# Sixteen working tiles lengthened by 32 bytes, so that they begin at different places modulo 512 bytes

## The chip, the cores and the metric

The kernel runs on one core of one Trainium2 chip. The metric is the device time of one execution in microseconds (us). Before the change it is 1171.81 us, the median of three runs (1171.26 to 1171.84). One further execution was taken with the hardware profiler; the rows below come from it.

## The reference

Two layers of a streaming encoder over 512 tokens of width 1024, in single precision. Layer 0 mixes tokens with differential attention, layer 1 with gated linear attention; both also attend to 256 memory tokens. Each layer ends in a gated MLP with a causal convolution:

```
for i in range(DEPTH):
    h = rms_norm(x, attn_norm[i])
    proj = h @ (w_in_diff or w_in_gla)
    mix = diff_attention(...) or gla_attention(...)
    cross = memory_cross_attention(mem_q, mem, ...)
    x = x + concatenate([mix, cross]) @ w_out[i]
    h = rms_norm(x, ffn_norm[i])
    x = x + (silu(g) * a) @ w_down[i]     # a, g: halves of conv(h @ w_up[i])
```

What matters here are the dense products: the input projection, the output projection, `h @ w_up` and the product with `w_down`.

## The kernel before, in words

**Split operands.** Every dense product is made of three matmuls. An operand is written as a rounded part `hi` (type fp32r) and the rest `lo`, and hi·hi + hi·lo + lo·hi is summed in one PSUM bank. `split` (L305) makes the pair of an activation, with ScalarE for `hi` and VectorE for `lo`; `split_weights` (L226) that of a weight tile.

**Which operand is loaded and which moves.** A matmul loads 128 columns of one operand into the array and lets up to 512 columns of the other move through.

- `gemm` (L327 to L329), the input projections: the loaded operand is a 128-column slice of the split tokens `xh[k]` or `xl[k]`; the weights `whi`, `wlo` move, 256, 272 or 512 columns wide. L507 is the same, written out for the first projection.
- `product` (L348 to L350), the output projection and the up projection: the loaded operand is a slice of the weights, and the tokens or the mixers' output move, 512 columns wide.
- the step of `down` (L1173), the down projection, done by a scheme of seven products: the loaded operand is a weight slice, and a middle tile of 256 columns moves. Two of the seven kinds of middle operand, b11 and t1, are made with `split_tiles()` and so lie in an x2 tile (`x` in the rows); the others are the pool tiles `midh`, `midl`.

**The x2 tiles.** Pool `xs` holds sixteen buffers with the tag `x2`, each two rows of 512 words a partition (4096 bytes): `pair` (L170) hands out the two rows, `split_tiles` (L174) gives one as `hi` and one as `lo`. Split tokens, split outputs of the mixers, the memory tokens, some operands of the linear attention, b11 and t1, and, from `load_x` (L1056), the residual stream `xT` all live there. In rows of the profile every one of them is called `x`. Beside them the pool has five tiles `xt`; pool `wp` has six `raw`, five `whi` and five `wlo` tiles of 4096 bytes, and the middle tiles have rows of 1024 bytes. Since all these sizes are multiples of 512 bytes, all these tiles begin at byte 416 modulo 512 of a partition, and so do their slices of 128 words. Exceptions are four weight tiles used once at the start (448), the constants `C` (128), the memory's keys and values (320), tiles of the linear attention with rows of 768 or 384 bytes, and the 272-column weight slices of one projection, which lie 1088 bytes apart.

**What sets the order.** TensorE's order is the program's own (`manual_schedule` at L162): attention and linear attention are written as steps, and `Filler` puts pieces of the dense products between them. Weights come as 128x1024 tiles on SP's queue two pieces or five tiles ahead, are split by ScalarE and VectorE, and are read by TensorE. The MLPs are dense products alone.

Of the kernel before, what the change touches and what calls it, by code (L numbers as in the profile page):

```python
# [11 lines left out]
F32 = mybir.dt.float32  # L12
# [9 lines left out]
S = 512  # L22
# [9 lines left out]
X2, XS, EM = 16, 5, 7  # L32
# [118 lines left out]
def trunk(ctx, tc, head_d, x_t, mem_t, wpack, cols_a_d, cols_d, conv_d, gate_d, rel_bias, diff_lambda, consts, onehot, out):  # L151
# [5 lines left out]
    xs = ctx.enter_context(tc.tile_pool(name="xs", bufs=1))  # L157
# [6 lines left out]
    def bank(tag):  # L164
        return ps.tile([128, 512], F32, name=f"ps_{tag}", tag=tag)

    def xtile():
        return xs.tile([128, S], F32, name="xt", tag="xs", bufs=XS)

    def pair(dt=F32):  # L170
        t = xs.tile([128, 2, S], dt, name="x2", tag="x2", bufs=X2)
        return t[:, 0], t[:, 1]

    def split_tiles(pool=None, tag=None, bufs=None):  # L174
        if pool is None:
            return pair(F32R)
        return (pool.tile([128, S], F32R, name=tag + "h", tag=tag, bufs=bufs),
                pool.tile([128, S], F32R, name=tag + "l", tag=tag, bufs=bufs))
# [174 lines left out]
    xT, xpair = [None] * KT, [None] * (KT // 2)  # L353
# [53 lines left out]

    tables("natural_log_exp_and_others")
    memT = [*pair(), *pair()]
    first = [bank("mm"), bank("mm"), bank("sm"), bank("sm")]  # L410

# [23 lines left out]
    with tc.tile_pool(name="ini", bufs=1) as ip, tc.manual_schedule(engines={E.Activation, E.DVE, E.Pool, E.SP}):  # L435
        idle = ip.tile([128, 512], F32, name="idle")
        rb = ip.tile([32, 6], F32, name="rb")
        oh = ip.tile([32, 640], F32, name="oh")
        bs = pair()
        bs = bs[0][:6], bs[1][:6, :128]  # L440
        lv = xtile()[:, :256]
        G.memset(idle, 0.0)
        p = bank("tp")
# [183 lines left out]
    def diff_layer(pool, mix, acc):  # L627
# [129 lines left out]
        for t in range(28):  # L757
# [15 lines left out]
            if t == 16:  # L773
                load_x(x_t)
                out_proj(0, mix, 0, None)
# [34 lines left out]
    def gla_layer(pool, mix, acc):  # L810
# [215 lines left out]
        for h in range(4):  # L1026
            scores(h)
            past_scores(h, 0)
            F.fill(f)
            past_scores(h, 1)  # L1030
            turn_keys(h)
            if h < 3:
                decays(h + 1)
            F.fill(f)
            states(h, 0)
            states(h, 1)
            if h < 3:
                products(h + 1)
            F.fill(f)
            if h == 2:  # L1040
                gate(0)
            outputs(h, 0)
            outputs(h, 1)
            group_norm(pool, o_[h], NB, 1, 192, True)
            F.fill(f)
            if h == 2:
                finish(0)
                load_x(xres)
                out_proj(1, mix, 0, None)
# [6 lines left out]
    def load_x(src):  # L1056
        for k in range(KT):
            if k % 2 == 0:
                xpair[k // 2] = xs.tile([128, 2, S], F32, name="x2", tag="x2", bufs=X2)
            xT[k] = xpair[k // 2][:, k % 2]  # L1060
            nc.sync.dma_start(xT[k], src[k])

# [319 lines left out]
```

## Time and profile before

| | before |
|---|---|
| median of 3 runs | 1171.81 us |
| profiled execution, its own time | 1170.8 us |
| its span, first to last instruction | 1168.9 us |
| TensorE busy with matmuls | 1155.8 us, 6448 matmuls |
| VectorE, ScalarE busy | 886.6 us, 599.2 us |
| DMA engines' mean share | 31.7% on the one busy queue |

How to read it: PE is TensorE's matmuls, PEld its weight loads, which overlap them; DVE is VectorE, ACT ScalarE, SP the queue that issues DMAs. L348 is line 348 of the kernel. `ps_mm<-x,whi 128*128 128x512` is a matmul that writes a bank `mm` from an x2 tile and a weight tile, 128 partitions by 128 loaded columns, 512 columns wide. A matmul's own duration (some 390 ns at 512 columns) says little, since the next one starts before it ends; what counts is the distance between starts.

### The profile page before, as it was taken

To read this page: it belongs to the slowest core of one execution; us is meant where nothing else is said; L and a number is where in the kernel's file an instruction comes from. 1 tells how busy PE (TensorE), PEld (TensorE's weight loads), DVE (VectorE), ACT (ScalarE), POOL (GpSimd) and SP (SyncE) were. 2 spreads that over 40 slices of the span, in tenths; PEclk is the share of its full clock that TensorE was granted. 3 is DMA by queue.
4 is the path that set the end of the run, shared out by engine and by line. 5 is a ranking of instruction groups with operands and counts; after the bars stand their busy time and mean duration, and the time that the engine had idled before them with its cause. 6 is when DMAs were issued, how large, how long until landed. Compare 5 with 4: busy or idle time off the path is not lost.

```text
span 1168.9 us, 16705 instructions
## 1 busy us (share of the span) xinstructions
PE 1155.8 (99%) x6448; PEld 988.7 (85%) x6448; DVE 886.6 (76%) x1454; ACT 599.2 (51%) x1048; POOL 4.1 (0%) x17
## 2 busy tenths in 40 slices
PE   9999999999999999999999999999999999999998
PEld 6887777788898889988998788988889988998888
DVE  7747687679886778668897746868998677876885
ACT  6856677566444444344467534536654344434441
POOL 0000000000000000000000000000000000000000
PEclk9999999999999999999999999999999999999999
DMA  9432213143225222522253221144221632253212
GB/s 313 162 97 90 68 55 127 59 129 97 64 70 182 91 73 72 162 93 70 66 169 112 73 73 46 55 153 126 86 68 64 189 99 73 72 155 98 72 37 73
DMA packets 39853, 117.94 MB, mean 101 GB/s; under 512 B 4735, under 2 KB 7608, under 8 KB 39774
## 3 DMA queue, kind: packets, MB, share of 16 engines
q1 hardware_dynamic: 39630, 116.62, 31.7%
q8 instruction: 51, 0.84, 0.3%
q14 instruction: 28, 0.23, 0.1%
q10 hardware_dynamic: 144, 0.26, 0.1%
HBM read 112.65 MB, written 4.21 MB: 100 GB/s over the span
## 4 chain that ended last, share of the span: by engine, by line
PE 91%; DVE 6%; ACT 2%; issue 1%; DMA 0%; DVEq 0%; ACTq 0%
PE ps_lg L1173 10%; PE ps_mm L348 9%; PE ps_mm L349 9%; PE ps_mm L350 9%; PE ps_sm L350 7%; PE ps_sm L348 7%; PE ps_sm L349 7%; PE ps_mm L327 5%; PE ps_mm L329 5%; PE ps_mm L328 5%; PE ps_tp L1173 5%; PE ps_mm L1173 3%; PE ps_tp L196 2%; PE ps_lg L686 1%; PE ps_sm L722 1%; DVE wlo L230 1%
## 5 line engine op out<-in xcount | busy, mean ns | idle before, releaser
L230 DVE TENSOR_TENSOR wlo<-raw,whi 128x1024 fp32r<-128x1024 f32 (+4 forms) x164 | 186.5, 1140 | 86.5 <-ACT whi L227 85.7
L227 ACT CAST whi<-raw 128x1024 fp32r<-128x1024 f32 (+4 forms) x164 | 160.7, 985 | 155.6 <-PE ps_sm L349 69.9
L348 PE MATMUL ps_mm<-x,whi 128*128 128x512 f32 x438 | 172.6, 394 | 0.3 <-DVE midh L1264 0.3
L349 PE MATMUL ps_mm<-x,whi 128*128 128x512 f32 x438 | 170.6, 389 | 0.2 <-DVE x L309 0.2
L350 PE MATMUL ps_mm<-x,wlo 128*128 128x512 f32 x438 | 170.6, 390 | 0.0
L348 PE MATMUL ps_sm<-x,whi 128*128 128x512 f32 x378 | 148.0, 392 | 0.0
L349 PE MATMUL ps_sm<-x,whi 128*128 128x512 f32 x378 | 147.1, 389 | 0.0
L350 PE MATMUL ps_sm<-x,wlo 128*128 128x512 f32 x378 | 147.1, 389 | 0.0
L327 PE MATMUL ps_mm<-whi,x 128*128 128x512 f32 (+2 forms) x336 | 132.0, 393 | 0.0
L329 PE MATMUL ps_mm<-whi,x 128*128 128x512 f32 (+2 forms) x336 | 126.6, 377 | 0.5 <-DVE x L309 0.4
L328 PE MATMUL ps_mm<-wlo,x 128*128 128x512 f32 (+2 forms) x336 | 125.9, 375 | 0.0
L263 ACT CAST whi<-raw 128x1024 fp32r<-128x1024 f32 (+1 forms) x60 | 58.3, 978 | 86.7 <-PE ps_sm L349 26.2
L348 PEld LDWEIGHTS ps_mm<-x,whi 128*128 128x128 f32 x438 | 82.3, 188 | 17.4 <-issue 0.9
L350 PEld LDWEIGHTS ps_mm<-x,wlo 128*128 128x128 f32 x438 | 82.2, 188 | 17.1
L349 PEld LDWEIGHTS ps_mm<-x,whi 128*128 128x128 f32 x438 | 82.3, 188 | 17.0 <-DVE x L309 0.6
L265 DVE TENSOR_TENSOR wlo<-raw,whi 128x1024 fp32r<-128x1024 f32 (+1 forms) x60 | 67.9, 1131 | 25.2 <-ACT whi L263 25.1
L349 PEld LDWEIGHTS ps_sm<-x,whi 128*128 128x128 f32 x378 | 71.0, 188 | 15.1 <-issue 0.5
L348 PEld LDWEIGHTS ps_sm<-x,whi 128*128 128x128 f32 x378 | 71.0, 188 | 15.0 <-issue 0.5
L350 PEld LDWEIGHTS ps_sm<-x,wlo 128*128 128x128 f32 x378 | 70.9, 188 | 14.8
L1173 PE MATMUL ps_lg<-midh,whi 128*128 128x256 f32 x264 | 75.0, 284 | 1.8 <-DVE x L1178 1.8
L1173 PE MATMUL ps_lg<-midl,whi 128*128 128x256 f32 x264 | 74.7, 283 | 0.0
L1173 PE MATMUL ps_lg<-midh,wlo 128*128 128x256 f32 x264 | 74.7, 283 | 0.0
(308 smaller groups left out, 2287.2 us busy)
## 6 DMA issues: line engine op xcount, KB each, us to landing
raw<-in_wpack_dram SPq DMA_DIRECT2D x170, 512.0 KB, 3.6
raw<-in_wpack_dram SPq DMA_DIRECT2D x24, 384.0 KB, 3.1
x<-in_x_t_dram SPq DMA_DIRECT2D x15, 256.0 KB, 5.2
xres<-x SPq DMA_DIRECT2D x8, 256.0 KB, 3.7
x<-xres SPq DMA_DIRECT2D x8, 256.0 KB, 5.1
raw<-in_wpack_dram SPq DMA_DIRECT2D x7, 256.0 KB, 5.4
bt<-bias_d SPq DMA_DIRECT2D x6, 256.0 KB, 4.9
x<-in_mem_t_dram SPq DMA_DIRECT2D x4, 256.0 KB, 6.1
```

The costliest lines, as they stand in the source:

```text
L196: nc.tensor.transpose(dst, src, ident[:n, :n])
L227: ins = A.copy(hi[:, c], raw[:, c])
L230: V.tensor_sub(lo[:, c], raw[:, c], hi[:, c].bitcast(F32))
L263: A.copy(hi[:, c], raw[:, c])
L265: todo = [lambda: V.tensor_sub(lo[:, c], raw[:, c], hi[:, c].bitcast(F32)), lambda: [sum_weights((*key[:3], *x)) for x in after]]
L327: mm(p, sh[k][:, blk(b)], hi, start=k == 0, stop=False)
L328: mm(p, sh[k][:, blk(b)], lo, start=False, stop=False)
L329: mm(p, sl[k][:, blk(b)], hi, start=False, stop=k == KT - 1)
L348: mm(p, hi[:, blk(n)], bh, start=i == first, stop=False)
L349: mm(p, hi[:, blk(n)], bl, start=False, stop=False)
L350: mm(p, lo[:, blk(n)], bh, start=False, stop=i == last)
L1173: mm(o, a[:, ws], b, start=start and (k, n, i) == (0, 0, 0), stop=k == last and i == 2, skip_group_check=True)
```

## The change

The sixteen x2 tiles get eight words more, 32 bytes, which nothing reads or writes. The view with two rows is cut from the first 1024 words, so each user sees the same shapes; `load_x`, which made such a tile by hand, uses the same function now.

```
     def xtile():
         return xs.tile([128, S], F32, name="xt", tag="xs", bufs=XS)

+    def two_tiles(dt=F32):
+        t = xs.tile([128, 2 * S + 8], dt, name="x2", tag="x2", bufs=X2)
+        return t[:, :2 * S].rearrange("p (a b) -> p a b", a=2)
+
     def pair(dt=F32):
-        t = xs.tile([128, 2, S], dt, name="x2", tag="x2", bufs=X2)
+        t = two_tiles(dt)
         return t[:, 0], t[:, 1]
...
     def load_x(src):
         for k in range(KT):
             if k % 2 == 0:
-                xpair[k // 2] = xs.tile([128, 2, S], F32, name="x2", tag="x2", bufs=X2)
+                xpair[k // 2] = two_tiles()
             xT[k] = xpair[k // 2][:, k % 2]
             nc.sync.dma_start(xT[k], src[k])
```

Buffer n of the sixteen then begins 32n bytes later than before: the sixteen begin at 416, 448, 480, 0, 32 and so on to 384 modulo 512 bytes, each at one place. Everything behind them moves by 16 x 32 = 512 bytes and keeps its place modulo 512. No instruction is added, left out or moved: on each of the five engines the same instructions stand in the same order, and only the line numbers behind the new function are four higher. The pools take 512 bytes more of each partition.

More of the change, by code (lines that the diff above doesn't have):

```diff
@@ L168, in xtile, with two_tiles @@
         return xs.tile([128, S], F32, name="xt", tag="xs", bufs=XS)
+    def two_tiles(dt=F32):
+        t = xs.tile([128, 2 * S + 8], dt, name="x2", tag="x2", bufs=X2)
+        return t[:, :2 * S].rearrange("p (a b) -> p a b", a=2)
     def pair(dt=F32):
-        t = xs.tile([128, 2, S], dt, name="x2", tag="x2", bufs=X2)
+        t = two_tiles(dt)
         return t[:, 0], t[:, 1]
@@ L1058, in load_x @@
             if k % 2 == 0:
-                xpair[k // 2] = xs.tile([128, 2, S], F32, name="x2", tag="x2", bufs=X2)
+                xpair[k // 2] = two_tiles()
             xT[k] = xpair[k // 2][:, k % 2]
```

## The prediction

> **What bounds the kernel now.** I read the head of the page and its busy times first, then the clock and the chain of work that ended last.
>
> ```profile
> span 1168.9 us, 16705 instructions
> PE 1155.8 (99%) x6448; PEld 988.7 (85%) x6448; DVE 886.6 (76%) x1454; ACT 599.2 (51%) x1048; POOL 4.1 (0%) x17
> ...
> core 0: 1168.9 us, clock 1.000
> ...
> PE 91%; DVE 6%; ACT 2%; issue 1%; DMA 0%; DVEq 0%; ACTq 0%
> ```
>
> TensorE is at work from one end to the other, at the full clock, and nine tenths of the chain that sets the end are its own instructions. So the span is the number of matmuls times the distance from one to the next, and that distance is what a change of addresses could touch. "Mean ns of one" does not give it, because matmuls overlap. I take it from starts. First the chain in order of time (start, us, what, count), in the down projection, whose matmuls are 256 columns wide:
>
> ```profile
> 1021.42 8.64 PE ps_lg L1173 x72
> ```
>
> 72 matmuls in 8.64 us are 120.0 ns each. Now TensorE's timeline in the up projection, 512 columns wide, where no row shows an idle time (first and last of a run of 85 matmuls):
>
> ```profile
> 381.38 0.39 PE L348 MATMUL ps_mm<-x,whi 128*128 128x512 f32 x1
> ...
> 400.42 0.39 PE L348 MATMUL ps_mm<-x,whi 128*128 128x512 f32 x1
> ```
>
> 84 distances in 19.04 us: 226.7 ns. The 256 extra columns cost 106.7 ns, so a column costs 0.417 ns, 512 columns 213.3 ns and 256 columns 106.7 ns. Both widths leave the same remainder, **13.3 ns per matmul**, 32 columns' worth. Every matmul has its weight load (6448 of each in the busy row), 128 columns deep; the remainder does not grow with the moving width, so it belongs to the load or to the change of weights. That is what the edit aims at.
>
> **The change part by part.** It removes and adds no instruction, and each engine's order is the same. Sixteen tiles of 4096 bytes become 4128 bytes, so tile n begins 32n bytes later. By the program's layout all sixteen, and whi, wlo and the mid tiles, begin at byte 416 modulo 512 before; after it the mid and weight tiles still do, and the x2 tiles stand at all sixteen multiples of 32. The halves of a tile (2048 bytes apart) and 128-column slices (512 bytes) keep their tile's place.
>
> How many matmuls have one operand in such a tile? The busiest groups, one row of each set:
>
> ```profile
> L348 PE MATMUL ps_mm<-x,whi 128*128 128x512 f32 x438 | 172.6, 394 | 0.3 <-DVE midh L1264 0.3
> ...
> L348 PE MATMUL ps_sm<-x,whi 128*128 128x512 f32 x378 | 148.0, 392 | 0.0
> ...
> L327 PE MATMUL ps_mm<-whi,x 128*128 128x512 f32 (+2 forms) x336 | 132.0, 393 | 0.0
> ...
> L1173 PE MATMUL ps_tp<-x,whi 128*128 128x256 f32 x176 | 32.3, 283 | 0.0
> L1173 PE MATMUL ps_lg<-x,whi 128*128 128x256 f32 x176 | 32.2, 283 | 0.0
> L1173 PE MATMUL ps_tp<-x,wlo 128*128 128x256 f32 x88 | 24.9, 283 | 0.0
> L1173 PE MATMUL ps_lg<-x,wlo 128*128 128x256 f32 x88 | 24.9, 283 | 0.0
> ```
>
> Lines 348 to 350 have the same counts, so 3 x (438 + 378) = 2448; lines 327 to 329 give 3 x 336 = 1008; the down projection 176 + 176 + 88 + 88 = 528. Together **3984**; the first projection (L507) and a few others add under 4% and are left out. One nanosecond per matmul is 4.0 us.
>
> What is a matmul's distance worth when its two streams begin at different places? The dense stages of before never show it, so I bound it by the two nearest stretches.
>
> First, the narrow projection of layer 1. Its weight pieces are 272 columns wide, so the slices begin 0, 1088 and 2176 bytes into whi: 0, 64 and 128 modulo 512 away from the x2 tile they meet.
>
> ```profile
> 611.59 0.29 PE L327 MATMUL ps_mm<-whi,x 128*128 128x272 f32 x1
> ...
> 614.48 0.29 PE L329 MATMUL ps_mm<-whi,x 128*128 128x272 f32 x1
> ```
>
> 24 matmuls, 23 distances, 2.89 us: 125.7 ns. 272 columns are 113.3 ns, so the remainder is 12.3 ns, 1.0 ns less than at equal places. This is the lower bound for places that have been seen: -1.0 ns.
>
> Second, a run just after TensorE has done something else (transposes or single-precision products). The places are equal, but the streams meet at another moment:
>
> ```profile
> 90.58 0.40 PE L328 MATMUL ps_mm<-wlo,x 128*128 128x512 f32 x1
> ...
> 92.89 0.39 PE L329 MATMUL ps_mm<-whi,x 128*128 128x512 f32 x1
> ```
>
> Eleven matmuls, ten distances, 2.31 us: 231.0 ns, 4.3 ns more than in the settled run, with no idle time between them. So the distance does depend on how the two streams stand to each other, and 226.7 ns is a state into which the kernel settles. With one place for all tiles every matmul repeats the last one's pattern; with another place every three matmuls (hi and lo of one tile serve three) it may not settle. Upper bound: +4.3 ns.
>
> The bounds are -1.0 and +4.3 ns. The stretches differ from the dense stages in width or in what ran before, neither is nearer, so I take the middle, **+1.65 ns**: 3984 x 1.65 = +6.6 us.
>
> [...]
>
> The other engines touch the same tiles. An operand at another place is in the trace: the first four raw tiles stand at byte 448 modulo 512.
>
> ```profile
> L230 DVE TENSOR_TENSOR wlo<-raw,whi 128x512 fp32r<-128x512 f32 x7 | 4.8, 681 | 0.0
> ...
> L1140 DVE TENSOR_TENSOR midl<-w,midh 128x512 fp32r<-128x512 f32 x22 | 15.1, 688 | 0.0
> L1140 DVE TENSOR_TENSOR x<-w,x 128x512 fp32r<-128x512 f32 x22 | 15.0, 683 | 0.7 <-ACT x L1137 0.7
> ```
>
> 681 against 683 and 688 ns: nothing, or 1% of operations that lie beside TensorE's matmuls (DVE has 6% of the chain; 1% of that is 0.7 us at most, either way). I take 0. The loads and stores of these tiles:
>
> ```profile
> x<-in_x_t_dram SPq DMA_DIRECT2D x15, 256.0 KB, 5.2
> xres<-x SPq DMA_DIRECT2D x8, 256.0 KB, 3.7
> x<-xres SPq DMA_DIRECT2D x8, 256.0 KB, 5.1
> ```
>
> Bytes, order and queue stay, the tiles were at no rounder place before (416), and DMA has 0% of the chain. Only the first seven loads of x have little cover, since TensorE waits for the first operands; half a microsecond either way is within the range. No wait is added anywhere.
>
> The profiled execution took 1170.8 us, 1.9 us around its span, and 1.0 us less than the median of 1171.8. So 1170.8 + 6.6 = 1177.4 us by the profile's own execution, **1178.4 us** as a median.
>
> **The rivals.**
>
> A, the forecast: the pattern is disturbed, each matmul costs -1.0 to +4.3 ns more; slower in most of that span, up to 1171.8 + 3984 x 4.3 ns = 1188.9 us. For it: 231.0 beside 226.7 ns. Against: the 272-wide stage, with places that do change, is no dearer.
>
> B, the place does not matter. The remainder is the same 32 columns at two widths, as a fixed price of changing weights would be, and 12.3 ns at mixed places is close to 13.3. Then nothing moves: 1171.8 us. [...]
>
> C, the other side: reads that begin at the same place collide, and apart they don't. Place: every matmul above. Price: what remains without collision. The nearest row is a transpose, whose operands begin 288 bytes apart (identity at 128, em at 416):
>
> ```profile
> 143.50 0.93 PE L196 MATMUL ps_tp<-C,em 128*128 128x128 f32 x7
> ...
> L196 PE MATMUL ps_tp<-C,em 128*128 128x128 f32 x92 | 14.0, 273 | 0.0
> ```
>
> (930 - 273) / 6 = 109.5 ns; a single-precision pass goes at two steps a column, and 2 x 128 x 0.417 is 106.7, so 2.8 ns remain. Relief is then 13.3 - 2.8 = 10.5 ns. With fifteen of sixteen places relieved that is 3984 x 15/16 x 10.5 = 39 us, 1133 us; if only the odd multiples of 32 are (the 272-wide stage has seen 64 and 128 and found no relief), 3984 x 8/16 x 10.5 = 21 us, 1151 us. It decides where two streams at full rate share something that repeats within 512 bytes. For it: the remainder is the same at 256 and 512 columns, as a collision over the 128 columns of a load would be. Against: 11 of these 13 ns stay at 64 and 128 bytes, and a run that meets at another moment costs more, never less.
>
> **How the numbers follow.** A 0.43 (0.07 of it above 1190, if a pattern that never settles is dearer than 231 ns), B 0.28, C 0.29 (0.10 of it below 1150). I count as no change what lies within 0.2%, 2.3 us, about what a measurement of this kernel tells from nothing. Likeliest is A at 1178.4 us. The range reaches up to 1190 (the upper bound) and down to 1150 (C with half the places relieved); it leaves out 0.17. Since it holds both signs: A's own range is 1174 to 1190. Faster 0.29, within 0.2% 0.28, slower 0.43.
>
> **What would show it.** After the change the chain's L1173 rows with mid operands must stay at 120.0 ns, since none of their operands moves: they are a control. A: the dense L348 run shows 227 to 231 ns, uneven from tile to tile; B: 226.7 ns as before; C: 216 to 222 ns. If those distances stand still and the time moves, I was wrong about the place, and DVE, ACT or the loads are to be read. The prediction is wrong altogether if distances fall at most places, for then the settled state of before was a collision and not the best one.

## The result and the profile after

The changed kernel takes 1187.80 us, the median of four runs (1187.64 to 1187.92); the kernel before took 1171.53 us beside it (four runs, 1170.90 to 1171.84). The ratio is **1.0137, with an interval of 1.0125 to 1.0150**: slower, by 16.3 us where 6.6 were forecast. The profiled execution took 1187.64 us, 1.8 us around its span.

The head of the page, and the shares of the chain that ended last:

```profile
span 1185.8 us, 16705 instructions
PE 1172.7 (99%) x6448; PEld 987.6 (83%) x6448; DVE 887.6 (75%) x1454; ACT 598.8 (51%) x1048; POOL 4.1 (0%) x17
...
PE 87%; DVE 8%; ACT 2%; DMA 1%; issue 1%; SPq 0%; DVEq 0%; ACTq 0%
```

The span grew by 16.9 us and PE's busy time by as much, 1155.8 to 1172.7 us, with the same 6448 matmuls. DVE (886.6 to 887.6) and ACT (599.2 to 598.8) did the same work in the same time. The groups that the forecast put at nothing did stay there (lines behind the new function are four higher; out<-in, shapes, count, busy us, mean ns; then the loads of the tokens):

```profile
L1144 DVE TENSOR_TENSOR x<-w,x 128x512 fp32r<-128x512 f32 x22 | 15.1, 684 | 0.7 <-ACT x L1141 0.7
```

```profile
x<-in_x_t_dram SPq DMA_DIRECT2D x15, 256.0 KB, 5.2
xres<-x SPq DMA_DIRECT2D x8, 256.0 KB, 3.7
```

683 ns became 684, and 5.2 and 3.7 us are what they were. So the time is in the distances between matmuls. TensorE's timeline in the up projection, whose weights are loaded while the x2 tiles move, first and last of a run of 130 matmuls with no idle time:

```profile
379.77 0.40 PE L353 MATMUL ps_mm<-x,whi 128*128 128x512 f32 x1
...
409.82 0.40 PE L353 MATMUL ps_mm<-x,whi 128*128 128x512 f32 x1
```

129 distances in 30.05 us: **232.9 ns** where it was 226.7. And the chain in the down projection (start, us, what, count): first the 48 matmuls whose middle operand is an x2 tile, then 24 whose middle operand lies in a middle tile:

```profile
456.61 2.83 PE ps_lg L1177 x24
459.44 2.84 PE ps_tp L1177 x24
462.28 2.87 PE ps_mm L1177 x24
465.14 2.88 PE ps_lg L1177 x24
```

2.88 us for 24 is 120.0 ns, the control that had to stand still. The x2 rows have 2.83 and 2.84, 118 ns: at 256 columns the new places are *better*. The row of 2.87 is where the one pattern passes into the other.

Summing all distances between one matmul's start and the next one's, by kind, from the two traces (us; each matmul's distance is the time to the next start):

| kind | matmuls | before | after | ns each |
|---|---|---|---|---|
| `product`, 512 columns, x2 moves (L352 to L354) | 2448 | 559.9 | 574.4 | +5.92 |
| `gemm`, 512 columns, x2 loaded (L331 to L333) | 864 | 204.8 | 207.4 | +3.06 |
| `gemm`, 272 and 256 columns, x2 loaded | 192 | 25.7 | 25.6 | -0.7 |
| down projection, 256 columns, x2 moves | 528 | 63.5 | 62.5 | -1.98 |
| down projection, middle tiles move (control) | 1319 | 160.8 | 161.0 | +0.2 |
| first projection (L511) | 96 | 22.4 | 23.4 | +10.9 |
| all others | 1000 | 126.1 | 125.9 | -0.2 |

Together +16.9 us, all of the span's difference. The first projection's 1.0 us is hardly the change's: it is there, by 1.0 and 1.1 us, in the runs midshift and mid192 below too, which leave these tiles where they were, so it seems that this one profile of before began faster.

### The profile page after: what moved, and what is told of

Read it like the earlier page. It is cut to its first block, busy times and chain, and to the rows that moved or that the text cites. A ratio compares the mean times of both kernels' runs of the same rounds, so it can differ in the third digit from the quotient of the medians.

```text
span 1185.8 us, 16705 instructions
## 1 busy us (share of the span) xinstructions
PE 1172.7 (99%) x6448; PEld 987.6 (83%) x6448; DVE 887.6 (75%) x1454; ACT 598.8 (51%) x1048; POOL 4.1 (0%) x17
## 4 chain that ended last, share of the span: by engine, by line
PE 87%; DVE 8%; ACT 2%; DMA 1%; issue 1%; SPq 0%; DVEq 0%; ACTq 0%
PE ps_mm L353 9%; PE ps_mm L352 9%; PE ps_mm L354 9%; PE ps_lg L1177 8%; PE ps_sm L353 8%; PE ps_sm L354 8%; PE ps_sm L352 8%; PE ps_mm L331 5%; PE ps_mm L332 5%; PE ps_mm L333 5%; PE ps_tp L1177 4%; PE ps_mm L1177 2%; PE ps_tp L200 2%; DVE wlo L269 1%; PE ps_lg L690 1%; PE ps_sm L726 1%
## 5 line engine op out<-in xcount | busy, mean ns | idle before, releaser
L352 PE MATMUL ps_mm<-x,whi 128*128 128x512 f32 x438 | 174.7, 399 | 0.1
L353 PE MATMUL ps_mm<-x,whi 128*128 128x512 f32 x438 | 173.3, 396 | 0.2 <-DVE x L313 0.2
L354 PE MATMUL ps_mm<-x,wlo 128*128 128x512 f32 x438 | 173.2, 395 | 0.0
L352 PE MATMUL ps_sm<-x,whi 128*128 128x512 f32 x378 | 150.0, 397 | 0.0
L354 PE MATMUL ps_sm<-x,wlo 128*128 128x512 f32 x378 | 149.5, 395 | 0.0
L353 PE MATMUL ps_sm<-x,whi 128*128 128x512 f32 x378 | 149.5, 395 | 0.0
L331 PE MATMUL ps_mm<-whi,x 128*128 128x512 f32 (+2 forms) x336 | 132.9, 396 | 0.0
L333 PE MATMUL ps_mm<-whi,x 128*128 128x512 f32 (+2 forms) x336 | 127.4, 379 | 0.5 <-DVE x L313 0.4
L352 PEld LDWEIGHTS ps_mm<-x,whi 128*128 128x128 f32 x438 | 82.3, 188 | 19.7 <-issue 0.6
L354 PEld LDWEIGHTS ps_mm<-x,wlo 128*128 128x128 f32 x438 | 82.2, 188 | 19.5
L352 PEld LDWEIGHTS ps_sm<-x,whi 128*128 128x128 f32 x378 | 71.0, 188 | 17.4 <-issue 0.5
L354 PEld LDWEIGHTS ps_sm<-x,wlo 128*128 128x128 f32 x378 | 70.9, 188 | 16.9
```

What stands on the lines that cost most here:

```text
L331: mm(p, sh[k][:, blk(b)], hi, start=k == 0, stop=False)
L333: mm(p, sl[k][:, blk(b)], hi, start=False, stop=k == KT - 1)
L352: mm(p, hi[:, blk(n)], bh, start=i == first, stop=False)
L353: mm(p, hi[:, blk(n)], bl, start=False, stop=False)
L354: mm(p, lo[:, blk(n)], bh, start=False, stop=i == last)
```

## The experiments

The forecast's reason was that a pattern is lost when the place changes every three matmuls. The theories set against each other, named by these letters where an expectation names them:

- **T1**, the forecast's: a *change* of place from tile to tile unsettles the stream. A constant difference costs nothing.
- **T2**: the distance depends on *how far apart* the moving and the loaded operand begin, and equal places are the good ones at 512 columns. Changing from tile to tile adds little.
- **T3**: it takes the traffic of the other engines or the DMAs to the same tiles.
- **T4**, the forecast's rival C: equal places collide. It had fallen for 512 columns with the result, but the down projection points its way.

**Run mb: the disputed cost by itself.** Behind the kernel before, 17 runs of 48 matmuls at 512 columns (96 at 256) on tiles that nothing else touches, at a time when the other engines are done. The pattern is the kernel's: hi·hi, hi·lo, lo·hi on one tile, then the next tile.

```
+        zero, step = lambda k: 0, lambda k: 8 * k % 128        # words
+        runs = (("warm", 512, zero, zero), ("a", 512, zero, zero),
+            ("b", 512, lambda k: 8, zero), ("c", 512, lambda k: 16, zero), ("d", 512, lambda k: 32, zero),
+            ("e", 512, lambda k: 64, zero), ("f", 512, step, zero), ("g", 512, zero, step), ("h", 512, step, step),
+            ("i", 512, lambda k: 64 * (k % 2), zero), ("j", 512, lambda k: 8 * (k % 2), zero),
+            ("k", 256, zero, zero), ("l", 256, step, zero), ("m", 256, zero, step), ("n", 256, lambda k: 8, zero),
+            ("o", 512, lambda k: 4 * k, zero), ("p", 512, lambda k: 64 * (k // 8), zero))
...
+                x, a, b = xt_[k % 8], mo(k), 128 * (k % 8) + lo_(k)
+                hi, lo, xh_, xl_ = (wt[:, b:b + 128], wt[:, 1024 + b:1152 + b],
+                                    x[:, a:a + w], x[:, 512 + a:512 + a + w])
```

The first function of a run gives the words by which the moving operand is shifted, the second those of the loaded one.

> The kernel before, with 17 runs of 48 matmuls added behind its last instruction, alone on the chip, so that a distance between starts can be read for each pattern of places (weights loaded from one tile, eight moving tiles, three matmuls a tile). Theory T1 (the settled state needs a repeating place; what costs is that an operand's place changes from one matmul to the next): runs a to e, with the moving operand 0, 32, 64, 128, 256 bytes away but always the same, all 226.7 ns; f (moving place steps by 32 bytes each tile) 233 ns, as in the kernel after; h (both step together) 233 too; i and j (two places in turn) 230 to 234; p (one change in the middle) 226.7 but for five or six matmuls; g (loaded place steps) 227 to 231. At 256 columns k 120 ns, l 118. Rival T2 (the distance depends on how far apart the two operands begin): b to e differ from a by 4 ns or more, h equals a. Rival T3 (the extra time of the kernel after is not TensorE's own but needs the other engines' traffic): all runs of 512 columns 226.7 ns.

The chain that ended last names each run of the bench and its length, so the mean distance is the length divided by the count:

```profile
1184.75 10.88 PE mb_a L1330 x48
1195.63 11.20 PE mb_b L1330 x48
...
1228.99 10.93 PE mb_e L1330 x48
1239.92 11.14 PE mb_f L1330 x48
1251.06 11.11 PE mb_g L1330 x48
1262.17 11.05 PE mb_h L1330 x48
1273.22 10.88 PE mb_i L1330 x48
...
1295.20 11.51 PE mb_k L1330 x96
1306.71 11.31 PE mb_l L1330 x96
...
1329.41 11.20 PE mb_n L1330 x96
```

Run a, equal places: 10.88 / 48 = 226.7 ns, the kernel's own number. Run b, always 32 bytes apart: 11.20 / 48 = 233.3 ns. Nothing changes from tile to tile in b, and it costs as much as run f, where the moving tiles step through all sixteen places (11.14, 232.1). So the difference alone is enough, and T1 is not needed. Run i, 0 and 256 bytes apart in turn, has the 226.7 ns of equal places (10.88), and run e, always 256, settles there after its first matmuls (10.93): 256 bytes apart counts as equal, half of the 512 that I had assumed. Run h steps both operands together: the difference stays zero, and it still costs 3.5 ns (11.05, 230.2), so a change of place has a price of its own, but a smaller one. At 256 columns the sign is the other one: 11.51 / 96 = 119.9 ns at equal places (k), 11.20 / 96 = 116.7 ns at 32 bytes (n). And no other engine is at work here (the last VectorE instruction of the chain, a fill of the bench's tiles, ends at 1178.3 us, run a begins at 1184.75), so T3 isn't needed either.

T2 does not come out as its expectation had it: run c (64 bytes, 11.00 us, 229 ns) costs some 2 ns and not 4, run e costs nothing once settled, and h does not equal a. What is kept of it below is a distance that depends on how far apart the operands begin, with 256 bytes the same as 0, and beside it a price for a change of place.

**Run shift32: one constant difference in the kernel.** The x2 tiles keep their length; an empty tile of 32 bytes ahead of their pool moves all sixteen (and the pool's five `xt` tiles with them), and 480 bytes behind it put the rest back at its place. Nothing steps from tile to tile any more.

```
+    pa = ctx.enter_context(tc.tile_pool(name="pa", bufs=1))
+    pa.tile([128, 8], F32, name="padfront")
     xs = ...
+    pb = ctx.enter_context(tc.tile_pool(name="pb", bufs=1))
+    pb.tile([128, 120], F32, name="padback")
```

> All sixteen x2 tiles stay at 4096 bytes and at one place, but 32 bytes away from the weights' place. T1 (changing places cost): 1171.5 us within 1 us, dense runs settle at 226.7 ns. T2 (unequal places cost): 1180 to 1190 us. T4, the opposite (reads that begin at the same place collide): 1150 us.

1188.56 us, ratio 1.0150 (1.0133 to 1.0167): as slow as the change. TensorE's timeline in the up projection, the first and the last of 135 matmuls:

```profile
379.63 0.39 PE L354 MATMUL ps_mm<-x,wlo 128*128 128x512 f32 x1
...
410.89 0.39 PE L353 MATMUL ps_mm<-x,whi 128*128 128x512 f32 x1
```

31.26 us for 134 distances is 233.3 ns, run b's number to the tenth. By kind: `product` +6.17 ns each, `gemm` at 512 columns +3.62, the x2 steps of the down projection -2.22, `gemm` at 272 columns 0.0. So T1 falls as the cause of the loss: all of it is there without any stepping.

**Run shift256: the same with 256 bytes** (64 words in front, 64 behind).

> As the shift by 32 bytes, but by 256, half of 512. T1: 1171.5 us within 1 us. T2: 1180 to 1190 us. T4: 1150 us.

1171.27 us, ratio 1.0002 (0.9992 to 1.0011). The up projection's timeline, first and last of 138 matmuls:

```profile
379.77 0.39 PE L354 MATMUL ps_mm<-x,wlo 128*128 128x512 f32 x1
...
410.83 0.39 PE L353 MATMUL ps_sm<-x,whi 128*128 128x512 f32 x1
```

31.06 / 137 = 226.7 ns. Moving the tiles is not what costs here; standing 32 bytes from the weights (233.3 ns) instead of a multiple of 256 (226.7) is. This is also the control for the two pads, which are in both kernels. By its number alone the run fits what T1 expected, and T2's 1180 to 1190 us were missed: T2 had been written for places that repeat every 512 bytes. It is the bench's runs e and i, which hold 226.7 ns at 256 bytes, that let T2 stand with 256.

**Run padw: the other operand.** The x2 tiles stay as they were before; the split weight tiles are 32 bytes longer instead (three places like this one, and 192 bytes behind the pool).

```
-        hi, lo = (wp.tile([128, WTILE], F32R, name=t, tag=t, bufs=WB) for t in ("whi", "wlo"))
+        hi, lo = (wp.tile([128, WTILE + 8], F32R, name=t, tag=t, bufs=WB) for t in ("whi", "wlo"))
```

> The weights' tiles are lengthened by 32 bytes and the x2 tiles stay: whi and wlo stand at five places each, 160 bytes apart from one another. In the up and output projections the loaded operand then changes its place at each switch between whi and wlo, in the input projections the moving one does. T1 in the narrow form (only the moving operand's place matters): the up projection stays at 226.7 ns, the input projections of 512 columns go to 231 to 235; 352 x 3 of them, +3 to +6 us in all, 1175 to 1178 us. T1 in the wide form (either operand's place): the up projection too goes to 231 or more, 1185 us or more. T2: about as the kernel after, 1188 us.

1181.48 us, ratio 1.0089 (1.0074 to 1.0104): `product` +4.50 ns each, `gemm` at 512 columns +2.67, and the down projection's two kinds -2.28 and -1.35, since now its middle tiles, too, begin elsewhere than the weights. No x2 tile has moved and the loss is there, so it belongs to the pair of operands and not to the token tiles (T2). Run g of the bench, with the loaded operand stepping, has 11.11 / 48 = 231.5 ns, +4.8, which agrees with the 4.5. The total was expected by no theory: it lies below T2's 1188 us and the wide T1's 1185, and above the narrow T1's 1178.

**Run mb2: all differences.** The bench with one constant difference in each run, 17 at 512 columns and 13 at 256.

```
+        wide = (0, 0, 1, 2, 4, 6, 8, 12, 16, 20, 24, 28, 32, 40, 48, 56, 60)      # words
+        narrow = (0, 2, 4, 8, 12, 16, 24, 32, 40, 48, 56, 60, 64)
```

> As the first added bench, with constant distances between the places of the moving and the loaded operand: 512 columns at 4 to 240 bytes, 256 columns at 0 to 256 bytes, 48 or 96 matmuls each. T2, as the first bench left it (the distance between starts is a function of how far apart the operands begin, modulo 256 bytes): 512 columns 226.7 at 0 only or nearly only, 233 at 32, 229 at 64, 232 at 128, most others 229 to 234; 256 columns 120.0 at 0 and at 256, 116 to 119 elsewhere. T1 (only a change of place costs): all runs of one width alike, which the first bench already speaks against.

The chain, for 0, 4, 8, 32 and 64 bytes at 512 columns, then 0, 32, 192 and 256 bytes at 256:

```profile
1185.20 10.88 PE mb_wb L1327 x48
1196.09 11.43 PE mb_wc L1327 x48
1207.52 11.20 PE mb_wd L1327 x48
...
1241.09 11.20 PE mb_wg L1327 x48
...
1263.48 11.00 PE mb_wi L1327 x48
...
1363.87 11.52 PE mb_na L1327 x96
...
1398.11 11.20 PE mb_nd L1327 x96
...
1466.15 10.90 PE mb_nj L1327 x96
...
1499.65 11.50 PE mb_nm L1327 x96
```

In ns per matmul, from the starts of each run without its first twelve matmuls:

| bytes apart | 0 | 4 | 8 | 16 | 24 | 32 | 48 | 64 | 96 | 128 | 160 | 192 | 224 | 240 |
|---|---|---|---|---|---|---|---|---|---|---|---|---|---|---|
| 512 columns | 226.7 | 238.3 | 233.3 | 231.6 | 234.6 | 233.3 | 233.4 | 228.8 | 233.2 | 232.4 | 234.3 | 233.3 | 233.3 | 233.3 |
| 256 columns | 120.0 | | 120.0 | 116.7 | | 116.7 | 118.3 | 117.8 | 120.0 | 118.7 | 117.3 | 113.3 | 118.3 | 117.1 |

At 512 columns zero is the best of all the places tried (80 and 112 bytes gave 231.1 and 231.3), next comes 64. At 256 columns zero is the worst, with 8, 96 and 256 bytes, and 192 bytes is the best: 113.3 ns, 6.7 ns over the 106.7 that 256 columns take by the prediction's estimate (226.7 - 120.0, from the trace of before). So T4 is wrong at one width and right at the other, and a rule that reads only "apart" or "together" is no rule. T2's expectation held but for 238.3 ns at 4 bytes, and for 120.0 at 8 and 96 bytes and 113.3 at 192 at the narrow width. Each difference was run once, after one beginning; the runs below show that another steady value is possible.

**Run midshift: the middle tiles 32 bytes on.** If T2 holds, the kernel of before has places to gain from: the down projection's middle tiles meet the weights at equal places, at 256 columns. An empty tile ahead of them in their pool; all x2 tiles as before.

```
         rB = xtile()
+        pool.tile([128, 8], F32, name="padfront", bufs=1)
```

> The kernel before with one empty tile of 32 bytes ahead of the middle tiles of the MLPs, so that midh and midl begin 32 bytes from the weights' place; x2 stays. T2: 1320 matmuls of 256 columns go from 120.0 to between 116.7 (bench) and 117.8 ns (as the two x2 kinds did after the shift by 32): -2.9 to -4.4 us, 1167 to 1168.5 us, faster than both kernels. T1: no change, 1171.2 us. A rival T5 (at 256 columns the weight load, not the reads, sets the pace, and 120 ns is its length): no change, 1171.2 us.

1169.40 us, ratio 0.9987 (0.9979 to 0.9996): faster by 1.6 us, though less than the bench's 116.7 ns would give. The middle steps gained 1.61 ns each over 1319 matmuls, 2.1 us. The chain in the down projection of layer 0:

```profile
358.66 2.12 PE ps_tp L1174 x18
...
455.73 2.83 PE ps_mm L1174 x24
458.56 2.83 PE ps_lg L1174 x24
```

2.12 / 18 and 2.83 / 24 are 117.8 ns: a steady pattern, but not the bench's. That is the first sign that a difference doesn't fix the distance. The total lies 1 us above T2's range; T1 and T5, which expected no change, fall with the interval below 1.

**Run shift64: the x2 tiles 64 bytes on**, the second-best place of the bench at 512 columns (16 words in front, 112 behind).

> All x2 tiles at one place 64 bytes from the weights'. T2: the bench's 228.9 beside 226.7 ns, 2448 matmuls of the up and output projections +2.2 ns and about half of that for the input projections: +5.4 + 1 = +6 us, 1176 to 1179 us. T1: 1171.2 us. If any distance but 0 were equally bad: 1188 us.

1185.09 us, ratio 1.0119 (1.0104 to 1.0135), a clear miss of the expectation: `product` cost +4.66 ns each where the bench had +2.2. Two stretches of its timeline, both in the up projection of layer 0, before its first down piece (the down projection is done in three pieces a layer) and right behind it (133 and 130 matmuls):

```profile
279.63 0.39 PE L352 MATMUL ps_sm<-x,whi 128*128 128x512 f32 x1
...
309.85 0.39 PE L352 MATMUL ps_mm<-x,whi 128*128 128x512 f32 x1
...
379.72 0.40 PE L352 MATMUL ps_mm<-x,whi 128*128 128x512 f32 x1
...
409.82 0.40 PE L352 MATMUL ps_mm<-x,whi 128*128 128x512 f32 x1
```

30.22 / 132 = 228.9 ns in the first, 30.10 / 129 = 233.3 ns in the second, both steady, with the same tiles' places and the same lines. One difference, two patterns. By the starts, what ran just before tells them apart here: the four stretches of the up projection that begin right behind a down piece, 1440 of the 2448 matmuls, hold 233.3 ns to their end, and in both layers the stretch before the first down piece holds 228.9.

**Run mid192: the best place at 256 columns**, the edit of midshift with 48 words instead of 8.

> The kernel before with an empty tile of 192 bytes ahead of the MLPs' middle tiles: midh and midl begin 192 bytes from the weights' place, where the second bench found 113.3 ns at 256 columns beside 120.0 at equal places. T2: up to 1320 x 6.7 ns = -8.8 us; since the steps with b11 and t1 in between stay at distance 0 and each switch costs some matmuls, -4 to -8.8 us, 1162.3 to 1167 us. T1 (only a change of place costs): 1171.1 us, no change. Rival T6 (the bench's 113.3 ns needs an idle chip): like the shift by 32 bytes, 1169 us.

**1165.81 us, ratio 0.9954 (0.9941 to 0.9966)**: faster than the kernel before and than the changed one. The middle steps gained 4.41 ns each, 5.8 us in all, and every dense kind with an x2 tile but the first projection stood within 0.1 us. The chain where layer 0's second down piece goes from the x2 steps, which are still at equal places, to the middle tiles:

```profile
449.66 2.87 PE ps_lg L1174 x24
452.54 2.88 PE ps_tp L1174 x24
455.42 2.74 PE ps_mm L1174 x24
458.15 2.72 PE ps_lg L1174 x24
460.88 2.72 PE ps_tp L1174 x24
```

120 ns for the x2 steps, then 114.2 while it settles, then 2.72 / 24 = 113.3 ns, the bench's value. So T6 falls: 113.3 ns needs no idle chip.

**Runs em6 and w64: both kinds of the down projection at once.** w64 moves the down weights instead, by 64 bytes the other way, so that the x2 steps gain too; the weight tiles get 64 words more. The room for that comes from one buffer less of `em` and from three small tiles held once instead of four times, which em6 has alone as w64's control.

```
-X2, XS, EM = 16, 5, 7
+X2, XS, EM = 16, 5, 6
...
-        raw, c = wsums[key[:4]][name], slice(0, n)
+        raw, hi, lo, c = wsums[key[:4]][name], hi[:, 16:16 + n], lo[:, 16:16 + n], slice(0, n)
```

> Control for the next: six instead of seven buffers for the attention's scores and three small tiles held once instead of four times, to make room; no place changes modulo 512 bytes. Expected 1171 to 1175 us: the dense products as before, layer 0's attention the same or some us longer.

> As the control, with whi and wlo tiles 256 bytes longer (so at two places 256 bytes apart), in which the down projection's weights begin 64 bytes later: all 1848 matmuls of the down projection, b11 and t1 too, then move 192 bytes (modulo 256) from their weights, without a switch inside a step. T2: 120.0 to 113.3 ns, -12.3 us against the control, 1159 to 1163 us, and the up projection at 226.7 although the weights stand at two places. T1: two places cost, 1180 us or more. T6: -3 us against the control.

em6: 1175.29 us, ratio 1.0031 (1.0018 to 1.0044), the price of the buffers. w64: 1170.73 us, ratio 0.9998 (0.9989 to 1.0007), 4.6 us less than em6 and not the 12.3 expected. The two traces lie 5.1 us apart, of which only 2.8 stand in the down projection; the rest is mostly in the input projections and layer 0's attention, and why those are shorter than in em6 is not shown. The up projection kept its 226.7 ns though the weight tiles now stand at two places 256 bytes apart, which agrees with run i. The down projection is the miss:

```profile
467.16 8.48 PE ps_lg L1175 x72
```

8.48 / 72 = 117.8 ns, and so in nearly every group of this kernel's chain, at the difference at which mid192 has 113.3. By the starts both values occur in both kernels: in w64 the stretch from 347 to 350 us, behind a short pause, settles at 113.4 ns, and in mid192 the one that begins at 1134.84 us, behind a wait, at 117.7.

**Run mb3: what decides between the patterns?** The bench once more, always at 64 bytes (512 columns) or always at 192 bytes (256 columns). What differs is what ran just before: a run at another difference, or one odd matmul of 64 to 384 columns.

```
+        runs = [("wa", 512, 0, 0), ("wb", 512, 0, 0), ("wc", 512, 16, 0), ("wd", 512, 8, 0), ("we", 512, 16, 0), ...
+        runs += [("na", 256, 0, 0), ("nb", 256, 48, 0), ("nc", 256, 8, 0), ("nd", 256, 48, 0), ("ne", 256, 16, 0),
+                 ("nf", 256, 48, 0)]
+        runs += [("n" + chr(103 + i), 256, 48, b) for i, b in enumerate((64, 96, 128, 160, 192, 256, 320, 384))]
...
+            if br:
+                mm(p[:, :br], wt[:, 0:128], xt_[0][:, d:d + br], start=True, stop=True, skip_group_check=True)
```

> The kernel before, with 29 added runs of matmuls at its end. Every run but the controls has one fixed difference of operand places: 64 bytes at 512 columns (runs wc, we, wg to wo), 192 bytes at 256 columns (nb, nd, nf to nn). They differ only in what came just before: a run at another difference (0, 32, 128 bytes wide; 0, 32, 64 bytes narrow), or one single odd matmul of 64, 96, 128, 160, 192, 256, 320 or 384 columns. Theory E1, what ran before decides which of several stable patterns is entered: the distances of the 64-byte runs fall on two values, 228.9 and 233.3 ns, each held through its run, and those of the 192-byte runs on 113.3 and 117.8 ns. Theory E2, the pattern belongs to the difference alone, and the kernels' other values come from something else that the bench does not have (other engines' traffic, the order of banks): all the 64-byte runs 228.9 ns and all the 192-byte runs 113.3 ns after a few matmuls. Controls wb and na (difference 0): 226.7 and 120.0 ns.

The chain: 192 bytes after a run at 0, at 32 and at 64 bytes, then after an odd matmul of 128 and of 160 columns:

```profile
1352.31 11.31 PE mb_nb L1331 x96
1363.62 11.20 PE mb_nc L1331 x96
1374.83 11.31 PE mb_nd L1331 x96
1386.13 11.31 PE mb_ne L1331 x96
1397.44 10.89 PE mb_nf L1331 x96
...
1431.22 10.96 PE mb_ni L1331 x96
1442.25 11.35 PE mb_nj L1331 x96
```

The same 96 matmuls on the same operands take 11.31 us (nb, nd: 117.8 ns) or 10.89 us (nf: 113.4 ns), each held to the end. nf came after a run at 64 bytes. Of the eight runs after an odd matmul, those of 128 and 384 columns settled at 113.3 ns and the other six at 117.8. So at 256 columns the difference alone does not decide, and E2 falls. The runs also write different banks of PSUM, and by the program's layout the three at 113.3 ns (nf and those after 128 and 384 columns) lie in two banks and the others in the other six. The bank alone does not decide either: run nj of mb2 (113.3 ns) and run nd here (117.8) write the same bank at the same difference. What is known to differ between those two is what ran before, as E1 has it. At 512 columns and 64 bytes all eleven runs settled at 228.8 or 228.9 ns, whatever came ahead: there E1's second value, shift64's 233.3, did not appear. None of them followed a run of 256-column matmuls, as shift64's dearer stretches do.

## Why the prediction came out as it did

**What bounds the kernel** was right: the 16.9 us of span are all in the distances between matmuls, and no other engine's busy time moved by more than 1.0 us.

**The mechanism**, that the distance depends on how the two streams stand to each other, and is best where the kernel had settled, was right at 512 columns: 226.7 to 232.9 ns in the up projection. Forecast A's sign for it, 227 to 231 ns and uneven from tile to tile, had the right direction, and 232.9 lies above its top.

**The term that was mis-sized is the +1.65 ns per matmul.** The first four rows of the table (48 matmuls more than the 3984 counted) sum to 14.5 + 2.6 - 0.1 - 1.0 = 16.0 us, 4.0 ns each. That lies within the bounds of -1.0 and +4.3 ns, but at the upper one, and the middle was the wrong choice. Two things failed in it. The lower bound came from the 272-wide stage, and it does not carry to 512 columns: shift32 left the 272-wide matmuls where they were (0.0 ns) while it cost the 512-wide ones 6.17 ns. Width decides even the sign, as the bench shows; I had taken the same 13.3 ns remainder at two widths to mean that width doesn't matter. And the upper bound was no bound: 231.0 ns came from a run at equal places that was still settling (in the trace of before its next six distances, up to 94.25 us, average 226.7), while settled runs at unequal places stand at 228.8 to 238.3 ns. With 5.9 ns for `product`, 3.1 for `gemm` and -2.0 for the down projection the sum is 2448 x 5.92 + 864 x 3.06 - 528 x 1.98 = +16.1 us, beside a measured loss of 16.3; the bench at its stepping places gives 232.1 - 226.7 = +5.4 ns and 117.8 - 120.0 = -2.2 ns for the first and the last (runs f and l).

**The reason given**, that changing place every three matmuls keeps the pattern from settling, fell as the cause. shift32 changes nothing from tile to tile and costs as much. The changed kernel is uneven, 230.3 to 235.7 ns from tile to tile in the up projection, but its mean of 232.9 ns is no dearer than shift32's 233.3, where the tiles lie between 233.0 and 234.0. A change of place alone has a price, 3.5 ns in run h, but it does not add to that of unequal places.

**Rival B**, no dependence, fell: the bench's runs a and b differ by 32 bytes between the two operands and take 226.7 and 233.3 ns. That the two reads share something is an inference, and no run shows what. With a weight load for every matmul, the lowest steady distance that any run showed at 512 columns was 226.7 ns.

**Rival C**, a collision at equal places that unequal ones relieve, was wrong for the 3312 matmuls of 512 columns, where equal places are the best. Its sign was right at 256 columns, where 528 matmuls gained 1.0 us and, by mid192, another 1319 can gain 5.8; that a collision is the reason is not shown, and 8 and 96 bytes apart are no better there than 0. The two steps a column of a single-precision pass, on which its price rested, agree with the trace of before: where the row sums are made (L1127), two passes of 512 columns take 1.02 us, of which the second is 592 ns, so they start 428 ns apart, beside 109.5 ns at 128 columns; that is 0.83 ns a column, twice 0.417.

**The other edits at nothing** (DVE, loads, order) were right, and so was the control at 120.0 ns.

**What stays open.** Which beginning leads to which pattern is seen in part only. In shift64 the 233.3 ns follow down pieces, whose matmuls are 256 columns wide; the bench, which gave 228.9 after every beginning tried, had no such run ahead of its wide ones, so that this is the reason is not shown. In mid192 every stretch that begins right behind an x2 step at 120.0 ns settles at 113.3; w64 has no such step, its down pieces begin behind the up projection and hold 117.8 until the first pause. That fits E1 and is no rule, and w64 differs from mid192 in its weight tiles too. That differences other than 0 repeat after 256 bytes was not tried one by one. What it is in the chip that makes 256 bytes count as 0 no trace shows.

## What to carry to other kernels

In this kernel, whose TensorE is busy for 99% of the span, all 16.9 us lay in the distances between matmul starts, and these depended on where the loaded and the moving operand begin relative to each other: read them from starts, by kind and by width, before a tile is made longer or a pool is moved. A pad between two pools is a cheap experiment; at 512 columns here equal places modulo 256 bytes were best, at 256 columns 192 bytes apart, and each width needs its own measurement, in the kernel itself, since a bench's value need not appear there. A bound taken from a stage of another width (in shift32 272 columns cost 0.0 ns, 512 columns 6.17), or from a run that has not settled (231.0 ns, then 226.7), was no bound here.

## What the runs showed of the hardware

- The distance between matmuls depends on the difference of the operands' start addresses: 226.7 ns at 0 and 256, up to 238.3 ns at 4 bytes, with 512 columns; 113.3 (192 bytes) to 120.0 ns (0 bytes) with 256 columns. That is five to six percent at either width, with no wait in any row.
- The order turns over with the width: 0 bytes is the best place tried at 512 columns (226.7 ns) and among the worst at 256 (120.0). The 272-column matmuls, which stand at several differences before and after, kept their mean in shift32 (0.0 ns).
- One difference can hold more than one steady distance: 113.3 or 117.8 ns at 192 bytes and 256 columns in the same kernel, and 228.9 or 233.3 ns at 64 bytes and 512 columns in shift64. At 192 bytes the same difference and the same bank gave 113.3 ns in run nj of mb2 and 117.8 in run nd of mb3; what is known to differ between those two is what ran before.
